# An MLP in rounds of 1024 inner channels, its up steps placed among another round's down steps

## The chip, the cores and the metric

The kernel runs on one core of a Trainium2 chip. The metric is the device time of one execution in microseconds; a run's time is the median over repeated executions on the same chip.

## The reference, cut to what matters

One layer on 256 tokens of width 2048, all in float32: a chunked gated linear attention mixer, then a squared-ReLU MLP with 8192 inner channels, then a last RMS norm.

```python
h = h + _gla_mixer(_rmsnorm(h, gla_norm[0]), ...)
a = jax.nn.relu(_rmsnorm(h, mlp_norm[0]) @ w_up)     # 256 x 8192
h = h + (a * a) @ w_down                             # 256 x 2048
return _rmsnorm(h, final_norm)
```

## The kernel before, in words

Every product is made from float32 split in two parts of the type float32r, a high part (ScalarE casts) and a low part (VectorE subtracts the cast from the value). A product is the sum of three matmuls: high by high, high by low, low by high. Nearly all matmuls are 128 x 128 by 128 x 256. Weights come from memory as raw tiles through SP's queue, 512 KB to a load; `parts` (or `weights`) splits a raw tile into a slot `hi` and a slot `lo`, of which there are five each. The raw tiles were held in three pairs.

The order of the instructions on each engine is fixed when the program is built, by a scheduler that follows the program's text and its own estimate of when things are ready; each engine then works its list in order and waits on semaphores. The list `side` holds small jobs that `pump` puts between the steps of the main loops.

The mixer takes about the first 375 us. Then the MLP follows in four rounds of 2048 inner channels (`ROUNDS = HID // D`):

- `up(r, q, act)`, four blocks of 512 channels. `turned` runs 8 steps (kp) for each block; a step loads 256 x 512 of `w_up` and makes 24 matmuls, with the weights as the stationary operand and the transposed hidden state (`hth`, `htl`) as the moving one. Then ReLU and square, and for each bank of 256 channels the eight forms of the activation that the down steps use: the four quarters A11, A12, A21, A22 (two token halves by two channel tiles) and the four combinations S1 to S4, split into high and low parts.
- `down(r, half, act)`, two half passes over 1024 of the 2048 output columns, each 8 steps (kp) over 256 channels. The left 512 columns go by sums: seven products of 256 columns in place of eight (Winograd's form of Strassen's scheme), for which VectorE forms four sums of the weights (`u`, three additions) that are split as well. The right 512 columns are plain, in 24 matmuls. `blocks` are the plain products, `product` the others. At the end of a half pass the banks are added into `h` (`take`) and into `sums`.

In the last round the second half pass is replaced by a plain loop over 16 channel tiles at the end, whose last six weights are held so that the output columns can be finished one after the other.

"Even" steps: TensorE's operands lie so that stationary tiles start at 192 bytes past a multiple of 256 (`OFF = 48`), moving ones at a multiple. In a step with `gap` set the second half of the weights is moved by 64 bytes:

```python
between = SLOT - OFF - 2 * GT if gap else 0
to = [a[:, OFF - between : OFF + 2 * GT + between].rearrange("p (i c) -> p i c", i=2)[:, :, between:] for a in to]
```

Of the kernel before, what the change touches and what calls it, by code (L numbers as in the profile page):

```python
# [27 lines left out]
F32 = mybir.dt.float32  # L28
# [33 lines left out]
ROUNDS = HID // D  # L62
# [5 lines left out]
def tile_gla_mlp(ctx, tc, x, xt, cols, w_vg, w_in, w_gate, w_out, w_up, w_down, final_norm, out):  # L68
# [7 lines left out]
    st = ctx.enter_context(tc.tile_pool(name="st", bufs=4))  # L76
# [37 lines left out]
    raw_half = []  # L114
# [5 lines left out]
    def weights(src, n, pieces=None, room=None, skip=0, raw=None, gap=None):  # L120
# [3 lines left out]
        if raw is None:  # L124
            if not raw_half:
                raw_half.extend(raw_pair())
            raw = raw_half.pop(0)
        loads, pieces = pieces or ([(0, n)], [(skip, n)])
# [43 lines left out]
    def turned(row, w, c0, even=(0,), acc=None):  # L172

        acc = acc or acc_banks(GT // P // 2)
        for kp in range(KT // 2):
            wh, wl = weights(w[2 * kp * P : 2 * (kp + 1) * P, c0 : c0 + GT].rearrange("(i p) c -> p i c", p=P), 2 * GT, gap=kp in even)
            for i in range(2):
                kt = 2 * kp + i
                ah, al = row(kt)
                for j in range(GT // P):  # L180
                    s = slice(j * P, (j + 1) * P)
                    o = acc[j // 2][:, j % 2 * T : (j % 2 + 1) * T]
# [6 lines left out]
                if kt < KT - 1:  # L189
                    pump()  # L190
        return acc
# [25 lines left out]
    mhalf = const.tile([P, 1], F32, name="mhalf")  # L217
# [18 lines left out]
    xe = mid.tile([P, 2, 2, P], F32R, tag="xe", name="xe")  # L236
# [98 lines left out]
    gn = const.tile([P, NT, GR], F32, name="gn")  # L335
# [19 lines left out]
    gt = mid.tile([GR, T], F32R, tag="gt", name="gt")  # L355
# [248 lines left out]
    sums = [big.tile([P, 4, T], F32, tag="E" + i, name="sums", bufs=1) for i in "hl"]  # L604
    turned_h = lambda kt: [a[:, kt, :].rearrange("p (t s) -> p t s", t=NT) for a in (hth, htl)]
# [30 lines left out]
    A11, A12, A21, A22, S3, S1, S2, S4 = range(8)  # L636
    KP = KT // 2
# [4 lines left out]
    def up(r, q, act):  # L642
        acc = turned(lambda kt: (hth[:, kt], htl[:, kt]), w_up, r * D + q * GT, even=() if q > 1 or r > 0 and q else (6,) if r == q == 0 else (0,))
        flush()
        f = work[:, 2].rearrange("p (f s) -> p f s", f=8)
        for b in range(2):
            s = tmp.tile([P, 2, T], F32, tag="t512", name="su", bufs=3)
            nc.vector.scalar_tensor_tensor(
                s, acc[b].rearrange("p (i t) -> p i t", i=2), 0.0, r2row.unsqueeze(1).to_broadcast([P, 2, T]),
                op0=ALU.max, op1=ALU.mult,  # L650
            )
            nc.scalar.activation(
                f[:, :4].rearrange("p (t i) s -> p i t s", t=2), s.rearrange("p i (t s) -> p i t s", t=2), AF.Square
            )
            sub = lambda o, x, y: nc.vector.tensor_tensor(o, x, y, op=ALU.subtract)
            sub(f[:, S3 : S1 + 1], f[:, A21 : A21 + 1].to_broadcast([P, 2, P]), f[:, A11 : A22 + 1 : 3])
            sub(f[:, S2], f[:, A11], f[:, S1])
            sub(f[:, S4], f[:, A12], f[:, S2])
            oh, ol = (act[q][:, b, i].rearrange("p f s -> p (f s)") for i in range(2))
            nc.scalar.copy(oh, work[:, 2])  # L660
            nc.vector.tensor_tensor(ol, work[:, 2], oh.bitcast(F32), op=ALU.subtract)

    def stationary(act, kp, f):
        return [act[kp // 2][:, kp % 2, i, f] for i in range(2)]
# [4 lines left out]
    def down(r, half, act):  # L669

        c0 = half * G
        plain = [aux_bank(), aux_bank()] if half == 0 else acc_banks(2)
        b32, b74 = acc_banks(2) if half == 0 else [aux_bank(), aux_bank()]
# [176 lines left out]
```

## Time and profile before

| | us |
|---|---|
| median of three runs | 1070.55 (1070.04 to 1071.04) |
| the profiled execution | 1070.33 |
| its span, first to last instruction | 1068.2 |
| TensorE busy in it | 1059.3 |
| VectorE busy | 780.7 |
| ScalarE busy | 579.9 |

The profile is of one execution. PE is TensorE, DVE VectorE, ACT ScalarE, POOL GpSimd, SP the engine that issues most loads. A row of the groups has the line, engine and operation, what is written and read, the count, then busy time and the mean duration of one in ns, then the idle time in front of them and what ended it. A row of the windows has a stretch of the span, its length, and for each engine its busy time and the number of instructions in it, then TensorE's granted clock, the DMA share and GB/s. A row of the timeline has start, duration, engine, line and operation. Matmuls overlap, so their own durations (0.28 us) say less than the distance of their starts.

### The profile page before, as it was taken

The page shows a single profiled execution, that of the slowest core. Times are in us where ns is not written, and L with a number is a line of the kernel's source. Part 1 is how long each engine was busy: PE and PEld are TensorE (multiplying, and loading weights), DVE is VectorE, ACT ScalarE, POOL GpSimd, SP SyncE. Part 2 cuts the span into 40 slices and gives each one's busy share as a digit, 9 for nine tenths or more (in the row PEclk, how much of TensorE's full clock was granted, in tenths as well). Part 3 has the DMA queues.
Part 4 walks back from the last instruction along what each step waited for, and adds up shares of the span by engine and source line. Part 5 has one row for each costly group of instructions (what it writes and reads, how often), then busy time and mean ns, then how long its engine had stood idle before and what let it go on. Part 6 is the DMA issues. An engine that isn't in the chain of part 4 may idle for free.

```text
span 1068.2 us, 21835 instructions
## 1 busy us (share of the span) xinstructions
PE 1059.3 (99%) x9262; PEld 1058.8 (99%) x9262; DVE 780.7 (73%) x1041; ACT 579.9 (54%) x701; POOL 12.8 (1%) x39
## 2 busy tenths in 40 slices
PE   9999999999999999999999999999999999999997
PEld 9999999999999999999999999999999999999996
DVE  5777645656555566789976689986779997778984
ACT  6775444546445455556654456554556554555652
POOL 0000000000000000000000000000000000000000
PEclk9999999999999999999999999999999999999999
DMA  9857665555555555556575655566655666665662
GB/s 340 301 165 233 195 191 155 161 150 178 198 179 179 196 172 186 195 167 228 198 236 183 198 174 200 198 223 211 198 197 165 196 233 217 193 192 177 219 227 79
DMA packets 79425, 210.43 MB, mean 197 GB/s; under 512 B 6704, under 2 KB 7600, under 8 KB 79200
## 3 DMA queue, kind: packets, MB, share of 16 engines
q1 hardware_dynamic: 78368, 206.99, 59.3%
q10 hardware_dynamic: 960, 2.05, 0.5%
q8 instruction: 72, 1.18, 0.4%
q14 instruction: 25, 0.20, 0.1%
HBM read 206.92 MB, written 2.10 MB: 196 GB/s over the span
## 4 chain that ended last, share of the span: by engine, by line
PE 98%; issue 1%; DVE 0%; ACT 0%; POOLq 0%; POOL 0%; DVEq 0%; ACTq 0%
PE acc L148 44%; PE acc L185 39%; PE aux L148 12%; PE aux L185 2%; PE aux L546 1%; PE aux L474 1%; PE aux L211 0%; PE acc L375 0%; DVE hf L809 0%; ACT sqf L762 0%; DVE h L667 0%; POOLq L846 0%; POOL rf L309 0%; PE aux L628 0%; DVEq L846 0%
## 5 line engine op out<-in xcount | busy, mean ns | idle before, releaser
L111 DVE TENSOR_TENSOR lo<-raw,hi 128x768 fp32r<-128x768 f32 (+3 forms) x226 | 257.0, 1138 | 120.2 <-ACT hi L110 118.1
L110 ACT CAST hi<-raw 128x768 fp32r<-128x768 f32 (+3 forms) x226 | 222.1, 984 | 214.0 <-PE acc L148 130.7
L185 PE MATMUL acc<-hh,hi 128*128 128x256 f32 x1024 | 283.2, 277 | 0.0
L185 PE MATMUL acc<-hl,hi 128*128 128x256 f32 x1024 | 283.2, 277 | 0.0
L185 PE MATMUL acc<-hh,lo 128*128 128x256 f32 x1024 | 283.1, 276 | 0.0
L137 DVE TENSOR_TENSOR lo<-raw,hi 128x1024 fp32r<-128x1024 f32 x160 | 195.3, 1223 | 110.1 <-ACT hi L136 109.0
L136 ACT CAST hi<-raw 128x1024 fp32r<-128x1024 f32 x160 | 167.9, 1051 | 181.1 <-PE acc L185 141.6
L148 PE MATMUL acc<-hi,act 128*128 128x256 f32 x1200 | 218.1, 276 | 0.0
L185 PEld LDWEIGHTS acc<-hh,hi 128*128 128x128 f32 x1024 | 192.3, 188 | 0.0
L185 PEld LDWEIGHTS acc<-hl,hi 128*128 128x128 f32 x1024 | 192.3, 188 | 0.0
L185 PEld LDWEIGHTS acc<-hh,lo 128*128 128x128 f32 x1024 | 192.3, 188 | 0.0
L148 PEld LDWEIGHTS acc<-hi,act 128*128 128x128 f32 x1200 | 180.9, 188 | 0.0
L148 PE MATMUL acc<-lo,act 128*128 128x256 f32 x600 | 143.3, 276 | 0.0
L148 PE MATMUL aux<-hi,act 128*128 128x256 f32 x704 | 133.8, 276 | 0.0
L148 PEld LDWEIGHTS aux<-hi,act 128*128 128x128 f32 x704 | 106.5, 188 | 0.0
L148 PE MATMUL acc<-hi,xA 128*128 128x256 f32 (+1 forms) x736 | 105.0, 280 | 0.0
L148 PEld LDWEIGHTS acc<-lo,act 128*128 128x128 f32 x600 | 102.5, 188 | 0.0
L148 PEld LDWEIGHTS acc<-hi,xA 128*128 128x128 f32 x736 | 94.0, 189 | 0.2 <-ACT hi L110 0.2
L110 ACT CAST hi<-work 128x1024 fp32r<-128x1024 f32 x56 | 59.1, 1056 | 38.3 <-PE aux L148 14.2
L148 PE MATMUL aux<-lo,act 128*128 128x256 f32 x352 | 76.4, 276 | 0.0
L111 DVE TENSOR_TENSOR lo<-work,hi 128x1024 fp32r<-128x1024 f32 x56 | 68.3, 1219 | 9.7 <-ACT hi L110 7.7
L148 PE MATMUL acc<-lo,xA 128*128 128x256 f32 (+1 forms) x368 | 58.6, 278 | 0.0
(162 smaller groups left out, 1271.8 us busy)
## 6 DMA issues: line engine op xcount, KB each, us to landing
raw<-in_w_up SPq DMA_DIRECT2D x128, 512.0 KB, 4.3
raw<-in_w_down SPq DMA_DIRECT2D x128, 512.0 KB, 4.4
raw<-in_w_in SPq DMA_DIRECT2D x80, 512.0 KB, 4.8
raw<-in_w_out SPq DMA_DIRECT2D x32, 512.0 KB, 4.1
raw<-in_w_vg SPq DMA_DIRECT2D x14, 520.0 KB, 8.8
h<-in_x SPq DMA_DIRECT2D x4, 512.0 KB, 7.6
zz<-in_xt SPq DMA_DIRECT2D x3, 384.0 KB, 8.5
fb<-in_final_norm ACTq DMA_DIRECT2D x1, 1024.0 KB, 6.8
```

What stands on the lines that cost most here:

```text
L110: last_hi[0] = nc.scalar.copy(hi[:, s], raw[:, s])
L111: last_lo[0] = nc.vector.tensor_tensor(lo[:, s], raw[:, s], hi[:, s].bitcast(F32), op=ALU.subtract)
L136: last_hi[0] = nc.scalar.copy(to[0], dst)
L137: last_lo[0] = nc.vector.tensor_tensor(to[1], dst, to[0].bitcast(F32), op=ALU.subtract)
L148: nc.tensor.matmul(o[:, m], x, w[:, m], start=first and c == 0, stop=last, skip_group_check=True)
L185: nc.tensor.matmul(o, u[:, i, s], m, start=kt == 0 and n == 0 and j % 2 == 0, stop=kt == KT - 1 and n == 2, skip_group_check=True,)
L474: nc.tensor.matmul(o, kab[:, k[0], c0 + c, k[1] : k[1] + P], q(qt[:, c0 + c]), start=c == 0, stop=c == 1)
L546: nc.tensor.transpose(b[:, o + t * P : o + (t + 1) * P], src[:, t, kt * P : (kt + 1) * P], ident)
```

## The change

The MLP goes in eight rounds of 1024 inner channels. `up` and `down` have become generators: 18 up steps run first (the first round's 16 and two more), and from then on each down step is followed by one up step of the next round, until the up steps are used up.

A down pass is now over one group of 512 output columns and one round (4 steps of 256 channels). A step is either plain (24 matmuls) or by sums (21) for all of its 512 columns; `by_sums` says which: three of four steps, two of four for group 1 and in the round before the last, and two steps in all in the last round. The groups are taken in one order and in the reverse in turn, so that the last group of one round is the first of the next and its four banks stay open. `sums` has four tiles instead of two; the small additions that end a group (`combine`) go to `side`. The first up block uses two of the six `acc` banks, the others the two `aux` banks.

There are six raw tiles of one step each instead of three pairs. The activation's forms are kept in another order, and those that no step uses are not made. Some small tiles are moved or padded in SBUF (`mhalf`, `gn`, `xe` and `gt` in one tile), which leaves the starts of TensorE's operands at the same offsets within 512 bytes. The plain loop at the end is over 8 channel tiles instead of 16. The even steps of the MLP are kp 6 and kp 0 of the first round's two blocks and kp 3 of each later round's first block.

```diff
-ROUNDS = HID // D
+MR = 2 * GT
+ROUNDS = HID // MR
...
-    st = ctx.enter_context(tc.tile_pool(name="st", bufs=4))
+    st = ctx.enter_context(tc.tile_pool(name="st", bufs=3))
...
-    def raw_pair():
-        a = wpool.tile([P, 2 * WMAX], F32, tag="raw", name="raw", bufs=3)
-        return a[:, :WMAX], a[:, WMAX:]
+    def raw_tile():
+        return wpool.tile([P, WMAX], F32, tag="raw", name="raw", bufs=6)
...
-    def turned(row, w, c0, even=(0,), acc=None):
-        acc = acc or acc_banks(GT // P // 2)
+    def turned_steps(row, w, c0, even, acc, flip=0):
         for kp in range(KT // 2):
...
+            yield
...
+    def by_sums(m, g, kp):
+        if m == ROUNDS - 1:
+            return (g, kp) in ((1, 0), (1, 2))
+        return kp < (2 if g == 1 or m == ROUNDS - 2 else 3)
+
+    def up():
+        for m in range(ROUNDS):
+            for q in range(MR // GT):
+                first = m == q == 0
+                acc = acc_banks(2) if first else [aux_bank(), aux_bank()]
+                even = (6,) if first else (0,) if m == 0 else (3,) if q == 0 else ()
+                yield from turned_steps(lambda kt: (hth[:, kt], htl[:, kt]), w_up, m * MR + q * GT, even, acc, 1)
...
+    def down(passes):
+        for n, (m, g) in enumerate(passes):
+            if not n or passes[n - 1][1] != g:
+                b32, bx4, b16, b57 = acc_banks(4)
+            ends = n + 1 == len(passes) or passes[n + 1][1] != g
+            for kp in range(KP):
...
+                raw = raw_tile()[:, : 2 * GT]
+                src = w_down[c0 : c0 + 2 * P, g * GT : (g + 1) * GT].rearrange("(i p) c -> p i c", p=P)
+                last_load[0] = nc.sync.dma_start(out=raw.rearrange("p (i c) -> p i c", i=2), in_=src)
+                if not by_sums(m, g, kp):
+                    w = parts(raw, 2 * GT, slots())
+                    for i in range(2):
+                        for bank, f in ((b32, (A11, A12)), (bx4, (A21, A22))):
+                            product(bank, slice(0, GT), at(f[i]), w, slice(i * GT, (i + 1) * GT))
+                    yield
+                    continue
+                w = parts(raw, 2 * GT, slots(), [(T, 2 * GT)])
...
+                add(u[:, :2], raw[:, :1].to_broadcast([P, 2, T]), raw[:, 1:3])
+                add(u[:, 2], u[:, 0], raw[:, 2])
+                add(u[:, 3], u[:, 2], raw[:, 3])
+                wu = parts(wk, G, slots())
+                product(b16, left, at(A11), w, block(1))
+                product(b32, right, at(A12), w, block(3))
+                product(b32, left, at(S4), w, block(2))
+                product(b57, left, at(S1), wu, block(0))
+                product(b57, right, at(S3), wu, block(1))
+                product(b16, right, at(S2), wu, block(2))
+                product(bx4, right, at(A22), wu, block(3))
+                yield
+            if ends:
+                take(b32, 0, g * GT, GT)
+                take(bx4, 1, g * GT, GT)
...
+    passes = [(m, g) for m in range(ROUNDS) for g in order_of(m) if m < ROUNDS - 1 or g < 2]
+    steps = up()
+    for _ in range(KT + 2):
+        next(steps)
+    for _ in down(passes):
+        next(steps, None)
...
-    acc = [acc_banks(len(cuts[t])) for t in range(NT)]
+    acc = [[aux_bank(), aux_bank()], acc_banks(3)]
+    KL = MR // P
...
-    for kt in range(KT):
+    for kt in range(KL):
```

More of the change, by code (lines that the diff above doesn't have):

```diff
@@ L640, in tile_gla_mlp @@
     work = work[:, : 3 * G].rearrange("p (b c) -> p b c", b=3)
[L642 to L654 removed]
+    acts = [[None] * (KP // 2) for _ in range(ROUNDS)]
```

189 lines of the change are left out of this document (87 added, 102 removed).

## The prediction

> **What bounds the kernel now.** I read the page from the top, then the chain that ended last, then windows over the MLP, then single rows of TensorE and of VectorE.
>
> ```profile
> span 1068.2 us, 21835 instructions
> PE 1059.3 (99%) x9262; PEld 1058.8 (99%) x9262; DVE 780.7 (73%) x1041; ACT 579.9 (54%) x701; POOL 12.8 (1%) x39
> ...
> 551.46 87.12 PE acc L185 x768
> ...
> 552.89:721.61 168.72, 168.72 (x1490) 168.72 (x1489) 138.20 (x182) 92.82 (x97) 0.00 (x0) 1.00 0.61 200
> 640.00:700.00 60.00, 60.00 (x532) 60.00 (x531) 59.00 (x84) 36.83 (x40) 0.00 (x0) 1.00 0.59 200
> ```
>
> TensorE is busy for 99% of the span. The chain shows 768 up-projection matmuls in 87.12 us without a wait, so one matmul costs 113.4 ns here. The first window is one whole round of before: 168.72 us hold the 1488 matmuls of 2048 channels (113.4 ns each), VectorE is busy for 138.2 us (82%). The second window lies in its down steps: VectorE 59.0 of 60, and TensorE still lost nothing. So time follows the number of matmuls, with VectorE close behind it.
>
> A second thing belongs to the bound: the pitch of the matmuls has two values.
>
> ```profile
> 383.85 1.03 PE L546 MATMUL aux<-ident,h 128*128 128x128 f32 x8
> ...
> 384.84 0.28 PE L185 MATMUL acc<-hl,hi 128*128 128x256 f32 x1
> ...
> 391.32 0.28 PE L185 MATMUL acc<-hh,lo 128*128 128x256 f32 x1
> ...
> 405.81 0.28 PE L185 MATMUL acc<-hl,hi 128*128 128x256 f32 x1
> ...
> 407.25 0.28 PE L185 MATMUL acc<-hl,hi 128*128 128x256 f32 x1
> ```
>
> After the eight short transposes at 383.85 the next 55 matmuls take 6.48 us, 117.8 ns each instead of 113.4, and stay so until an "even" step, whose shifted half runs 12 matmuls in 1.44 us (120 ns, the last two rows); behind it the pitch is 113.4 again. So an interruption of TensorE costs its own length and then 4.4 ns on every matmul up to the next even step. The MLP of before has no such interruption after its first up block.
>
> **The change, part by part.**
>
> *Matmuls.* A plain step over 256 channels and 512 columns has 4 x 2 x 3 = 24 matmuls, one by sums 21. Before, 7 half passes of 8 steps are by sums: 56. After, rounds 0 to 5 have 3+2+3+3 = 11 steps by sums of 16, round 6 has 8, round 7 has 2: 76. Twenty more steps save 3 matmuls each: 60, and the order of the built programs agrees (9228 to 9168). 60 x 113.4 ns = **-6.80 us**. All of them lie on the path, since TensorE is it.
>
> *Even steps.* Five in the MLP before (one of kp 6, one of the first round's second block, one in each of three rounds), nine after. Each costs 12 x (120 - 113.4) = 0.08 us: **+0.32 us**.
>
> *VectorE.* It gets the work that TensorE loses, so I count a round of 1024 channels of after.
>
> ```profile
> L137 DVE TENSOR_TENSOR lo<-raw,hi 128x1024 fp32r<-128x1024 f32 x160 | 195.3, 1223 | 110.1 <-ACT hi L136 109.0 <-PE aux L546 0.6
> L111 DVE TENSOR_TENSOR lo<-work,hi 128x1024 fp32r<-128x1024 f32 x56 | 68.3, 1219 | 9.7 <-ACT hi L110 7.7
> L111 DVE TENSOR_TENSOR lo<-raw,hi 128x768 fp32r<-128x768 f32 x56 | 53.4, 953 | 4.6 <-ACT hi L110 3.4
> L700 DVE TENSOR_TENSOR work<-work,raw 128x256 f32<-128x256 f32 x112 | 46.7, 417 | 0.2
> L700 DVE TENSOR_TENSOR work<-raw 128x512 f32<-128x512 f32 x56 | 38.3, 684 | 1.5 <-DMA raw<-in_w_down 1.3
> L648 DVE SCALAR_TENSOR_TENSOR su<-acc,work 128x512 f32<-128x512 f32 x32 | 21.1, 688 | 0.0
> L655 DVE TENSOR_TENSOR work<-work 128x128 f32<-128x128 f32 x64 | 18.6, 290 | 1.6
> L655 DVE TENSOR_TENSOR work<-work 128x256 f32<-128x256 f32 x32 | 13.4, 418 | 0.0
> L667 DVE TENSOR_TENSOR h<-acc,h 128x512 f32<-128x512 f32 x13 | 8.7, 684 | 7.2 <-PE acc L148 7.2
> L136 ACT CAST hi<-raw 128x1024 fp32r<-128x1024 f32 x160 | 167.9, 1051 | 181.1 <-PE acc L185 141.6 <-issue 17.5 <-PE acc L148 17.1
> L110 ACT CAST hi<-raw 128x768 fp32r<-128x768 f32 x56 | 47.0, 839 | 56.4 <-PE aux L148 27.9 <-PE acc L148 15.2 <-PE acc L185 13.3
> ...
> 993.52 1.22 DVE L111 TENSOR_TENSOR lo<-raw,hi 128x1024 fp32r<-128x1024 f32 x1
> 994.66 0.42 DVE L700 TENSOR_TENSOR work<-work,raw 128x256 f32<-128x256 f32 x1
> 994.99 1.22 DVE L111 TENSOR_TENSOR lo<-work,hi 128x1024 fp32r<-128x1024 f32 x1
> ```
>
> A step by sums costs 953 + 684 + 2 x 417 + 1219 = 3.69 us of vector instructions, a plain or an up step 1.22. Sixteen up steps 19.6, eleven by sums 40.6, five plain 6.1; the four activation banks 9.8 (four times 688, three times 418 + 2 x 290, and low parts of 896, 896, 1024 and 512 columns, the first two put at 1.09 us, halfway between the 768 and 1024 rows); three group ends of four 512-column additions, 8.2. Sum 84.3 us in 105 instructions. TensorE has 384 + 231 + 120 = 735 matmuls = 83.3 us. But queued vector instructions start before the one in front has ended: the last three rows start 1.14 and 0.33 us apart where they last 1.22 and 0.42, so each gives 0.08 us back. 84.3 - 105 x 0.082 = **75.7 us of 83.3**. Between the two ways of counting, the round of before (148.8 us by durations, 133.9 by starts) showed 138.2. I take the starts, as the lower bound of what VectorE needs when it is pressed: it is not the bound by itself, with 7.6 us to spare per round.
>
> The Trainium skill ("VectorE: DVE Perf Modes", section "The DRAIN you can't avoid") says the next operation does not start until the pipe has emptied; by that the need would be the full 84.3. The same page (section "Two Vector instructions with no wait between them") says that one that is not held starts earlier, and the rows above agree with that.
>
> *The raw tiles: what eats the spare 7.6 us.* The adds of a step by sums read the raw tile itself, and the order of the built program puts the first of them three to four steps ahead. That tile's buffer was freed only shortly before, by the low split of the load six tiles back, and the load that fills it waits in SP's queue for that split. I summed the vector work between the two, in starts: before, at least 4.2 us in all 56 cases, and VectorE waited 1.3 us for DMA in all (row L700 above). After: under 2 us in 3 of 76 cases, 2 to 3 in 27 (two splits of 1.14, for instance), 3 to 4 in 20, more in 26. Against this stands the landing time of a load.
>
> ```profile
> L133 SPq DMA_DIRECT2D raw<-in_w_up x1: 368/368/368, 567.4 to 567.4; - x1
> ...
> DMA to landing us min/median/max: 3.7/3.7/3.7
> ...
> DMA to landing us min/median/max: 3.7/4.2/4.6
> ...
> DMA to landing us min/median/max: 3.5/4.2/6.0
> ```
>
> The first two are one load of the pair issued at 567.4, the third both loads of that pair, the fourth all loads between 552.89 and 721.61. Before frees two raw tiles at once and issues in pairs, and the second of a pair lands last (4.6). After frees them singly, so I take the first's 3.7 us (its rows are of 2 KB, as those of w_down become), and 0.1 us for issue and wake-up. Adding up max(0, 3.8 - work) over the eleven adds of a round gives 4.9 to 6.8 us of waiting by round: 75.7 + 6.8 = 82.5 at most, still under 83.3, with under 1 us to spare. At a landing of 3.9 it is even; at the median 4.2 (4.3 with wake-up) the waits are 8.4 to 11.2 us and the round 84.1 to 86.9, over TensorE's 83.3. While VectorE waits at an add, the splits behind it wait too, and TensorE lives on the five weight slots.
>
> The Trainium skill ("DMA: Bandwidth & Descriptors", section "Anatomy of one DMA — SWDGE (gpsimd) path") gives 2.0 us and the bytes at 436 GB/s, 3.2 us for such a load as an estimate; here 3.5 is the shortest, and by 3.2 the waits would be no danger. Its "Rules for kernel authors" speak against the change: issue early, wait late. Here the wait moves closer to the issue, and the result hangs on it.
>
> Some loads land late (6.0 in the last row). I allow one that reaches TensorE: about 0.5 us, and half a round at the slow pitch, 367 x 4.4 ns = 1.6 us. Zero to **+2.1 us**; I take half, 1.05.
>
> *Hand-offs.* Up blocks now share two aux banks: the next block's first matmul waits for the two ReLU instructions (2 x 0.61 us in starts), with a down step of at least 21 x 113.4 ns = 2.4 us between. A new column group writes its b16 into the bank of the last b32, which one addition (0.60) must have emptied, with an up step (2.7 us) between. Both are covered while VectorE keeps pace; without that cover each of some 38 places costs up to 1.2 us.
>
> *At nothing.* ScalarE: 16 + 5 casts of 1051 ns, eleven pairs of 839 and 1051, and some 6 us for the activations make 49 us of a round's 83.3. Loads and bytes stay as many. The steps ahead of the MLP keep their order but for one raw load moved ahead of an input load; TensorE idles 8.9 us in the whole span (1068.2 - 1059.3), most of it at both ends, so I put the bounds at -0.5 and +0.5 us. The end keeps its last six held weights and the chain behind the last matmul, but only two steps instead of ten stand ahead of them: from the last group's start TensorE takes 90 + 48 + 30 matmuls, 19.1 us, until it wants the last split; VectorE has two steps by sums, two plain ones, eight splits and four additions there, 2 x 3.28 + 10 x 1.14 + 4 x 0.60 = 20.4 us in starts, and comes with a lead of up to five slots (five splits, 5.7 us). Covered; 1.3 us if the lead is gone.
>
> Sum: -6.80 + 0.32 + 1.05 = -5.43 us. The profiled execution took 1070.33 us (2.1 outside its span), so 1064.9 by its own time; the median of the runs is 1070.55, 0.2 above: 1070.55 - 5.43 = **1065.1 us**.
>
> **The rivals.** *The loads decide, in most rounds.* If a single load takes 4.2 us as the median does, VectorE falls behind, TensorE pauses at the group starts, and each pause drops the pitch until the round's one even step; then a round takes up to 735 x 117.8 ns = 86.6 us instead of 83.3. Over seven rounds at half to full effect +11.5 to +23 us, less 6.5: 1075.5 to 1087. It decides from a landing of about 4.0 us. For it: the median 4.2. Against: the first of a pair, 3.7. *The same in two to four rounds only:* +4 to +9 less 6.5, 1068 to 1073. *The pipe empties after each vector instruction:* 84.3 + 4.9 to 6.8 of waits is 89 to 91 us a round against 83.3, +6 to +8 in each of seven, 1105 to 1119. The start times speak against it. (It is the rule of the Trainium skill's "VectorE: DVE Perf Modes" weighed above.) *The change doesn't do what it says:* each of the 23 group ends pauses 0.3 us and returns the 6.8, 1070; no such wait showed at before's seven half passes.
>
> **How the numbers follow.** Forecast 0.60; loads in most rounds 0.20; in some 0.15; the last two 0.05 together. This kernel's measurement tells 0.2% (2.1 us) from no change. Faster by more means under 1068.4: the forecast and half of the third, 0.67. Within: the rest of the third and the 1070 case, 0.11. Slower 0.22. The range runs from 1063.3 (no late load, the early part 0.5 better) to 1075, the lower end of the loads' case, and leaves out about 2 in 10.
>
> **What would show it.** 9202 matmul records; a whole round of 83 to 84 us; VectorE at 94% or more there; waits of the adds for DMA of about 5 us a round where before had 1.3 in all. Wrong, if the chain shows TensorE waiting on VectorE in the MLP, if 60 us there hold about 512 matmuls (117.8 ns) where the second window above has 532, or if the landing of w_down loads has a median over 4.0 us.

## The result, and the profile after

The changed kernel takes 1079.49 us (median; 1077.17 to 1084.84), the kernel before 1070.32 in the same runs: ratio 1.0091, 95% interval 1.0069 to 1.0114. It is slower by 9.2 us where 5.4 us less were forecast. The profiled execution is the slowest of the six, 1084.84 us, 14.5 above the one of before; what follows from its trace is about that execution, and the median's 9.2 us were not traced.

The page of the changed kernel: span, busy times, the chain by engine and line, the groups of TensorE's up and down matmuls and of the adds, and the loads with their median time to landing.

```profile
span 1082.5 us, 22093 instructions
PE 1068.2 (99%) x9202; PEld 1066.8 (99%) x9202; DVE 831.1 (77%) x1144; ACT 587.9 (54%) x723; POOL 12.8 (1%) x39
PE 83%; DMA 7%; DVE 7%; issue 2%; ACT 0%; SPq 0%; DVEq 0%; POOLq 0%; POOL 0%; ACTq 0%
...
L180 PE MATMUL aux<-hh,hi 128*128 128x256 f32 x960 | 266.5, 278 | 2.8 <-DVE su L676 2.8
...
L143 PE MATMUL acc<-lo,act 128*128 128x256 f32 x908 | 223.0, 278 | 2.2 <-DVE lo L112 2.2
...
L736 DVE TENSOR_TENSOR work<-raw 128x512 f32<-128x512 f32 x76 | 52.5, 690 | 48.0 <-DMA raw<-in_w_down 47.7
...
raw<-in_w_up SPq DMA_DIRECT2D x128, 512.0 KB, 3.8
raw<-in_w_down SPq DMA_DIRECT2D x128, 512.0 KB, 4.3
```

The 60 matmuls are gone (9262 to 9202). The busy share still says 99%, and it hides the loss: a matmul at the slower pitch counts as busy. What is new is DMA and VectorE in the chain, 48 us of waiting at the first add of the steps by sums (1.5 us before), and TensorE waiting for `su` (the ReLU that empties an aux bank) and for low parts, 5 us in all.

Windows of 60 us over the changed kernel's MLP, TensorE first with its matmuls:

```profile
460.00:520.00 60.00, 59.30 (x505) 59.10 (x504) 53.38 (x74) 35.02 (x42) 0.00 (x0) 1.00 0.62 194
520.00:580.00 60.00, 60.00 (x529) 60.00 (x528) 52.95 (x72) 33.83 (x38) 0.00 (x0) 1.00 0.63 197
...
640.00:700.00 60.00, 60.00 (x512) 60.00 (x511) 53.91 (x75) 33.31 (x37) 0.00 (x0) 1.00 0.66 197
...
880.00:940.00 60.00, 57.82 (x492) 57.42 (x491) 53.15 (x76) 32.02 (x35) 0.00 (x0) 1.00 0.62 191
940.00:1000.00 60.00, 60.00 (x512) 60.00 (x511) 50.33 (x68) 31.49 (x35) 0.00 (x0) 1.00 0.63 192
```

Two windows here are full and still hold only 512 matmuls, whose starts are 117.8 ns apart, with the granted clock at 1.00 (two or three of the 512 lie partly outside). Two have real pauses. How two of them come about, in VectorE's timeline of the changed kernel and in TensorE's rows behind the pauses:

```profile
886.58 0.69 DVE L736 TENSOR_TENSOR work<-raw 128x512 f32<-128x512 f32 x1 [3.27 <-DMA raw<-in_w_down]
887.19 1.22 DVE L132 TENSOR_TENSOR lo<-raw,hi 128x1024 fp32r<-128x1024 f32 x1
...
891.27 1.28 DVE L760 TENSOR_TENSOR sums<-acc,sums 128x512 f32<-128x512 f32 x2
892.47 1.22 DVE L112 TENSOR_TENSOR lo<-raw,hi 128x1024 fp32r<-128x1024 f32 x1
895.45 0.69 DVE L736 TENSOR_TENSOR work<-raw 128x512 f32<-128x512 f32 x1 [1.76 <-DMA raw<-in_w_down]
896.06 1.22 DVE L132 TENSOR_TENSOR lo<-raw,hi 128x1024 fp32r<-128x1024 f32 x1
897.19 1.28 DVE L676 SCALAR_TENSOR_TENSOR su<-aux,work 128x512 f32<-128x512 f32 x2
```

```profile
888.46 0.38 PE L180 MATMUL aux<-hh,lo 128*128 128x256 f32 x1 [0.16 <-DVE lo L132]
...
897.93 0.38 PE L180 MATMUL aux<-hh,hi 128*128 128x256 f32 x1 [2.02 <-DVE su L676]
```

The first add stands 3.27 us for its load, the split behind it is late, and TensorE pauses 0.3 us at 888.1; from there on its matmuls come at the slower pitch. The second add stands 1.76 us. Behind it are a split and the two ReLU instructions without which TensorE may not write the aux banks again: TensorE pauses 2.2 us at 895.7, and the pitch stays slow. All five pauses of over 0.3 us in this trace are like that: TensorE is let go by a split or by `su`, and 1.9 to 2.5 us earlier VectorE began an add that had waited 0.8 to 3.3 us for a load of `w_down`.

Nearly the whole loss of the profiled execution lies in the MLP and can be added up from the starts of its matmuls. "MLP" is from its first up matmul to the end of the last matmul: 680.57 us before, 694.31 after, +13.74. The matmuls and even steps give -6.80 + 0.32. Five pauses (two starts over 0.3 us apart; the pause is what goes beyond one pitch) make 6.0, smaller ones 0.6, and 3232 matmuls at the slower pitch where before had 137 make 3095 x 4.45 ns = 13.8: sum 13.9. Another 0.5 us is lost ahead of the MLP.

### The profile page after: what moved, and what is told of

Read it like the earlier page. It is cut to its first block, busy times and chain, and to the rows that moved or that the text cites. A ratio compares the mean times of both kernels' runs of the same rounds, so it can differ in the third digit from the quotient of the medians.

```text
span 1082.5 us, 22093 instructions
## 1 busy us (share of the span) xinstructions
PE 1068.2 (99%) x9202; PEld 1066.8 (99%) x9202; DVE 831.1 (77%) x1144; ACT 587.9 (54%) x723; POOL 12.8 (1%) x39
## 4 chain that ended last, share of the span: by engine, by line
PE 83%; DMA 7%; DVE 7%; issue 2%; ACT 0%; SPq 0%; DVEq 0%; POOLq 0%; POOL 0%; ACTq 0%
PE acc L143 45%; PE aux L180 26%; PE acc L180 8%; DMA raw<-in_w_down 5%; DVE lo L112 3%; PE aux L143 2%; DVE lo L132 1%; DVE work L736 1%; DMA raw<-in_w_vg 1%; PE aux L549 1%; DMA zz<-in_xt 1%; DVE h L698 1%; PE aux L477 1%; DVE sums L760 0%; DVE su L676 0%
## 5 line engine op out<-in xcount | busy, mean ns | idle before, releaser
L143 PE MATMUL acc<-hi,act 128*128 128x256 f32 x1816 | 319.4, 278 | 0.0
L143 PEld LDWEIGHTS acc<-hi,act 128*128 128x128 f32 x1816 | 269.9, 188 | 0.0
L180 PE MATMUL aux<-hh,hi 128*128 128x256 f32 x960 | 266.5, 278 | 2.8 <-DVE su L676 2.8
L180 PE MATMUL aux<-hh,lo 128*128 128x256 f32 x960 | 266.7, 278 | 0.2 <-DVE lo L132 0.2
L180 PE MATMUL aux<-hl,hi 128*128 128x256 f32 x960 | 266.5, 278 | 0.0
L143 PE MATMUL acc<-lo,act 128*128 128x256 f32 x908 | 223.0, 278 | 2.2 <-DVE lo L112 2.2
L180 PEld LDWEIGHTS aux<-hh,hi 128*128 128x128 f32 x960 | 180.1, 188 | 3.2 <-DVE su L676 3.2
L180 PEld LDWEIGHTS aux<-hh,lo 128*128 128x128 f32 x960 | 180.3, 188 | 0.4 <-DVE lo L132 0.4
L180 PEld LDWEIGHTS aux<-hl,hi 128*128 128x128 f32 x960 | 180.2, 188 | 0.0
L736 DVE TENSOR_TENSOR work<-raw 128x512 f32<-128x512 f32 x76 | 52.5, 690 | 48.0 <-DMA raw<-in_w_down 47.7
L736 DVE TENSOR_TENSOR work<-work,raw 128x256 f32<-128x256 f32 x152 | 63.9, 420 | 1.0
L143 PEld LDWEIGHTS acc<-lo,xA 128*128 128x128 f32 x368 | 49.8, 188 | 0.3 <-DVE lo L112 0.3
```

The costliest lines, as they stand in the source:

```text
L143: nc.tensor.matmul(o[:, m], x, w[:, m], start=first and c == 0, stop=last, skip_group_check=True)
L180: nc.tensor.matmul(o, u[:, i, s], m, start=kt == 0 and n == 0 and j % 2 == 0, stop=kt == KT - 1 and n == 2, skip_group_check=True,)
L736: add = lambda o, x, y: nc.vector.tensor_tensor(o, x, y, op=ALU.add)
```

## The experiments

The theories named in the expectations: A, the loads of `w_down` land later than the adds want them; VectorE waits with what is queued behind, TensorE pauses and goes on at the slower pitch. B, VectorE has too much work, whatever it waits for. C, the slower pitch comes from the interleaving. D, the six single tiles are the cause. E, a late load stops TensorE whatever VectorE's spare time. In the table the median is of all runs and the rest is from that kernel's profiled execution, which lies up to 5.4 us from its median: the adds' wait for DMA in the whole kernel, the pauses of TensorE over 0.3 us and the matmuls at the slower pitch, both in the MLP, and its length. "Raw 4 + 2" means four raw tiles for `w_down` and two for `w_up`. The freeing split of a load is VectorE's last reading of the raw tile that the load will overwrite.

| kernel | median, us | adds' wait | pauses, us | slow matmuls | MLP, us |
|---|---|---|---|---|---|
| before | 1070.3 | 1.3 | 0 | 137 | 680.6 |
| changed | 1079.5 | 47.7 | 5, 6.0 | 3232 | 694.3 |
| adds later | 1091.9 | 0 | 13, 6.0 | 3686 | 698.1 |
| more even steps | 1077.9 | 49.8 | 6, 8.2 | 921 | 688.5 |
| no even steps | 1085.9 | 40.9 | 2, 1.0 | 4566 | 694.6 |
| raw pairs | 1073.7 | 44.4 | 1, 0.8 | 1841 | 683.0 |
| raw 4 + 2 | 1069.7 | 20.1 | 2, 0.7 | 1416 | 680.6 |
| raw 4 + 2, more even | 1068.4 | 21.9 | 1, 1.4 | 291 | 676.8 |
| sums not added | 1086.4 | 49.4 | 4, 5.2 | 2921 | 692.0 |
| 58 steps by sums | 1096.9 | 66.8 | 10, 7.2 | 3882 | 705.2 |
| raw 3 + 2 | 1082.3 | 44.9 | 4, 5.1 | 2984 | 694.0 |
| four slots, raw 5 + 3 | 1073.7 | 1.6 | 0 | 501 | 675.9 |
| five then four slots, raw 5 + 3 | 1072.1 | 2.1 | 0 | 192 | 674.4 |
| five then four slots, raw 3 + 3 | 1094.9 | 60.6 | 6, 3.2 | 4977 | 700.3 |
| the last but one, fifth slot aligned | 1065.9 | 1.8 | 0 | 135 | 674.1 |

**The adds later.**

```diff
+                before = last_lo[0]
                 w = parts(raw, 2 * GT, slots(), [(T, 2 * GT)])
 ...
+                with tc.issue_after(before.ins):
                     add(u[:, :2], raw[:, :1].to_broadcast([P, 2, T]), raw[:, 1:3])
                     add(u[:, 2], u[:, 0], raw[:, 2])
                     add(u[:, 3], u[:, 2], raw[:, 3])
```

> The three adds of a by-sums step are put behind the split that VectorE did just before this step's own; at least 8.0 us of vector work (by the durations of the trace) then lies between the split that frees a raw tile and the first add on its new content, where it was 1.1 to 7.2 us. Work and sums are the same. Theory A (the loads land later than the early adds want them, VectorE waits with its splits queued behind, TensorE pauses and falls to the slower pitch): the adds' waits for w_down fall from 47.7 us to under 3, no pause of TensorE over 0.3 us is left in the MLP, the pitch stays at 113.4 ns, and the time is the prediction's sum, 1064 to 1066 us. Theory B (VectorE has too much work with 20 more steps by sums, whatever it waits for): 1077 to 1080 us, unchanged. Theory C (the slower pitch comes from the interleaving of up and down steps itself): pauses go, the 117.8 ns stretches stay, about 1073 us.

Measured 1091.9 us (1.0188, 1.0167 to 1.0210): none of the three. The waits for DMA are gone as built, and others are in their place. VectorE's two longest waits between 440 and 960 us in the changed kernel (us, times, longest), the longest in this one, and a piece of this one's timeline:

```profile
DVE work L736 <- DMA raw<-in_w_down: 44.8, 41, 3.3
DVE lo L112 <- ACT hi L111: 13.1, 15, 2.0
```

```profile
DVE lo L112 <- ACT hi L111: 46.7, 53, 1.2
```

```profile
590.16 0.88 DVE L737 TENSOR_TENSOR work<-work,raw 128x256 f32<-128x256 f32 x2
591.56 1.40 DVE L676 SCALAR_TENSOR_TENSOR su<-aux,work 128x512 f32<-128x512 f32 x2 [0.53 <-PE aux L180]
592.88 1.22 DVE L112 TENSOR_TENSOR lo<-work,hi 128x1024 fp32r<-128x1024 f32 x1
```

The split of the sums now stands right behind the adds that make them (68 of 76 with under 1.2 us of vector work between, 39 in the changed kernel), so VectorE waits for ScalarE's cast, 46.7 us where it was 13.1, and TensorE's pauses end with ScalarE's casts (8) or with splits (5). The early place of the adds had a use; taking a wait away by moving its instruction only moved it. This run does not decide between A and B, and A's own figure missed as well.

**More even steps, and none.**

```diff
-                even = (6,) if first else (0,) if m == 0 else (3,) if q == 0 else ()
+                even = (6,) if first else (0,) if m == 0 else (3,)
```

> One more even step in each round from the second on, in the second half of the up steps (seven in all, 12 matmuls at 120 ns each, 0.08 us a step); order and sums unchanged. Theory A: the adds' waits (about 48 us) and the pauses (five, about 6.5 us in all) stay, but a slow stretch ends about 42 us earlier; of the 3084 slow matmuls of the profiled run some 750 to 1300 are left, that is 8 to 10 us less than in that run and, since it was the slowest of six, 5 to 9 us less than the median: 1071 to 1075 us. Theory B: the time stays at 1077 to 1080 us, whatever the pitch, since TensorE would only wait longer for VectorE.

and with `()` in place of `(3,) if q == 0 else ()`:

> The even steps of the rounds from the second on are taken out (seven); order and sums unchanged. Theory A: after the first pause, near 465 us, TensorE stays at 117.8 ns to the end: some 5000 slow matmuls instead of 3084 in the profiled run, 8 to 10 us more than that run, less 0.56 us for the even steps: 1086 to 1093 us. Theory B: 1077 to 1080 us, unchanged.

Measured 1077.94 us (1.0075, 1.0062 to 1.0087) and 1085.86 (1.0149, 1.0134 to 1.0165). With more even steps the slow matmuls fall to 921 as expected, but the median falls by 1.6 us and not by 5 to 9, and the two intervals overlap. In the two traces, both of executions above their medians, the MLP is 5.8 us shorter: the pitch gives back 2311 x 4.45 = 10.3 us, the added even steps cost 0.6, the pauses grow from 6.0 to 8.2 us, and behind the longest of them the granted clock is at 0.50 for 3.4 us, about 1.5 us more. That TensorE waits longer because it wants its weights sooner at the faster pitch is likely, not shown.

Without even steps the pitch falls at 551.9 us and never comes back; TensorE's rows there, and two windows:

```profile
551.50 0.28 PE L143 MATMUL acc<-lo,act 128*128 128x256 f32 x1
551.65 0.39 PE L180 MATMUL aux<-hh,hi 128*128 128x256 f32 x1
551.88 0.28 PE L180 MATMUL aux<-hl,hi 128*128 128x256 f32 x1
```

```profile
460.00:520.00 60.00, 60.00 (x532) 60.00 (x532) 54.59 (x76) 37.49 (x43) 0.00 (x0) 1.00 0.63 200
760.00:820.00 60.00, 60.00 (x512) 60.00 (x512) 53.30 (x74) 34.03 (x38) 0.00 (x0) 1.00 0.64 193
```

The two starts at 551.65 and 551.88 are late by 0.16 us together. That is no pause by the table's limit, and it was enough; the two pauses of the table, 1.0 us together, come later, when the pitch is already slow. The median lies just under the 1086 to 1093 expected. So the price of the pitch is real (4566 slow matmuls, 20 us), and it follows pauses, very short ones too, and not the interleaving: up to 551 us up and down steps alternate here at 113.4 ns (against C).

**Raw tiles in pairs again.**

```diff
-        return wpool.tile([P, WMAX], F32, tag="raw", name="raw", bufs=6)
+        if not raw_half:
+            a = wpool.tile([P, 2 * WMAX], F32, tag="raw", name="raw", bufs=3)
+            raw_half.extend((a[:, :WMAX], a[:, WMAX:]))
+        return raw_half.pop(0)
```

> One part of the change undone: the raw weight tiles are three pairs again and not six single tiles, so loads are issued two at a time, once both tiles are free; sums and rounds as in the changed kernel. In the built order 40 of the 76 by-sums steps have under 4 us of vector work between the freeing split and the first add (2.0 to 7.3 us in all). Theory A: the adds still wait, 40 to 60 us in all, and the time stays within 1074 to 1082 us. Rival D (the six single tiles are what made the loads late): the waits are near 2 us, as in the kernel before, and the time is 1064 to 1067 us.

Measured 1073.72 us (1.0033, 1.0021 to 1.0046). That is 0.3 us under A's range. The adds still wait 44 us, so D falls; but there is one pause over 0.3 us instead of five, and three of 0.1 to 0.3 us at which the pitch fell. How much is waited doesn't tell where it is waited.

**Four raw tiles for `w_down`, two for `w_up`.**

```diff
-        return wpool.tile([P, WMAX], F32, tag="raw", name="raw", bufs=6)
+        n_raw[0] += 1
+        down = kind == "down" if kind else n_raw[0] % 6 < 4
+        return wpool.tile([P, WMAX], F32, tag="raw" + "ud"[down], name="raw", bufs=4 if down else 2)
```

(`kind` is "down" or "up" in the MLP and none ahead of it, where the six take turns.)

> The six raw tiles are shared out by kind in the MLP: four for w_down and two for w_up (in the changed kernel the two kinds take turns, three each). Work, sums, even steps and bytes are the same. In the built order 15 of the 76 by-sums steps have under 4.0 us of vector work between the freeing split and the first add (50 in the changed kernel), and 61 have over 4. Theory A (a round on VectorE is its work, some 76.5 us, and its waits for loads, 8.2 us: 85 us against TensorE's 83.3, so TensorE is made to pause): the adds' waits fall from 47.7 to 15 to 25 us, a round of VectorE to under 81 us, the pauses go, and the time is 1064 to 1067 us. Theory B (VectorE's work alone is too much, and waits only take the place of other idling, as with the late adds): the waits turn up elsewhere on VectorE and the time stays over 1073 us.

> The last kernel with one more even step in each round from the second on (0.08 us each, 0.56 us in all). Theory A: without pauses there is nothing to repair, so 0.3 to 0.6 us more than the kernel with four and two; if one or two pauses are left, up to 3 us less. Theory B: as the kernel with four and two, over 1073 us.

Measured 1069.73 us (1.0004, 0.9989 to 1.0018) and 1068.37 (0.9986, 0.9975 to 0.9996). Same memory, work and bytes as the changed kernel, and 9.8 us less: fewer late loads, fewer pauses. It misses 1064 to 1067 by what two pauses of 0.7 us together leave behind, 1279 slow matmuls more than before had, 5.7 us; with the added even steps 291 are left, and one pause of 1.4 us at 967.

**VectorE relieved, loads left late; and fewer steps by sums.**

```diff
-                    if g not in begun:
-                        nc.scalar.copy(dst, b)
-                    else:
-                        nc.vector.tensor_tensor(dst, b, dst, op=ALU.add)
+                    nc.scalar.copy(dst, b)
```

> VectorE is relieved and the loads are left as they are: the sums' banks are copied by ScalarE in every round and not added by VectorE in rounds after the first, so this kernel leaves out the accumulation of the sums over the rounds (its output is not the reference's; TensorE's work is unchanged). VectorE loses two adds of 128x512 a group, some 5 us a round. In the built order the adds stand as close behind their loads as in the changed kernel or closer (56 of 76 with under 4.0 us of vector work). Theory A: the adds' waits stay at 45 to 65 us, but a round of VectorE is 80 to 82 us and TensorE does not pause for it: 1064 to 1068 us. Rival E (one late load stops TensorE directly, whatever VectorE's spare): pauses stay and the time is 1074 us or more.

```diff
-        return kp < (2 if g == 1 or m == ROUNDS - 2 else 3)
+        return kp < 2
```

> The number of by-sums steps is taken back nearly to what it was, in every group two of four: 58 steps instead of 76, so 54 matmuls more, 6.1 us, and some 2.5 us of vector work less for each step not taken, 6 to 7 us a round. The adds stand closer behind their loads than in the changed kernel (44 of 58 with under 4.0 us of vector work). Theory A: the waits stay near 8 to 12 us a round, but VectorE has 70 us of work, so a round is 80 to 82 us of TensorE's 84.2: few pauses and 1069 to 1072 us. Rival E: pauses as before, 1080 us or more.

Measured 1086.44 us (1.0144, 1.0127 to 1.0160) and 1096.92 (1.0256, 1.0234 to 1.0279). Both are far over A's figures, and on E's side; the first of them leaves out the adding of the sums over the rounds. The busy times of the kernel that doesn't add the sums, a piece of VectorE's timeline in it, and the page of the kernel with 58 steps by sums:

```profile
PE 1066.0 (99%) x9202; PEld 1064.6 (99%) x9202; DVE 812.4 (75%) x1106; ACT 607.0 (56%) x761; POOL 12.8 (1%) x39
```

```profile
722.76 0.69 DVE L736 TENSOR_TENSOR work<-raw 128x512 f32<-128x512 f32 x1 [3.31 <-DMA raw<-in_w_down]
723.37 1.22 DVE L132 TENSOR_TENSOR lo<-raw,hi 128x1024 fp32r<-128x1024 f32 x1
724.51 0.42 DVE L736 TENSOR_TENSOR work<-work,raw 128x256 f32<-128x256 f32 x1
724.84 1.28 DVE L676 SCALAR_TENSOR_TENSOR su<-aux,work 128x512 f32<-128x512 f32 x2
```

```profile
PE 1078.9 (99%) x9256; PEld 1076.2 (98%) x9256; DVE 787.5 (72%) x1054; ACT 573.0 (52%) x705; POOL 12.8 (1%) x39
...
L736 DVE TENSOR_TENSOR work<-raw 128x512 f32<-128x512 f32 x58 | 40.1, 691 | 66.9 <-DMA raw<-in_w_down 66.8
```

VectorE has 19 and 44 us less to do than in the changed kernel (831.1), and TensorE still pauses 5.2 and 7.2 us, where it was 6.0. In the first kernel the relief was smaller than the 5 us a round that I had put down (38 additions less, 19 us in all). But B falls: the kernel with the least vector work is the slowest, and the last kernel below has 836.5 us of it and no pause. In the rows at 722 the add waits 3.31 us, since the split in front of it is the one that freed its tile; two instructions on stands `su`, and TensorE pauses 2.7 us there. What VectorE has to spare over a round does not help at that place: `su` can't be done ahead, because its bank is full only when TensorE has ended the up block, one down step before TensorE wants the bank again.

**Five raw tiles, three and two.**

```diff
-        return wpool.tile([P, WMAX], F32, tag="raw", name="raw", bufs=6)
+        n_raw[0] += 1
+        down = kind == "down" if kind else n_raw[0] % 5 < 3
+        return wpool.tile([P, WMAX], F32, tag="raw" + "ud"[down], name="raw", bufs=3 if down else 2)
```

> Five raw tiles instead of six: three for w_down, as many as in the changed kernel, and two for w_up. In the built order the distances of the adds are those of the changed kernel to within a tile or two (49 of 76 with under 4.0 us of vector work, 50 there). If the adds' loads decide and w_up's third tile buys nothing: waits of the adds 42 to 52 us, four to six pauses, 1077 to 1083 us. If the number of raw tiles as such decides: clearly slower than the changed kernel, 1085 us or more.

Measured 1082.26 us (1.0113, 1.0099 to 1.0126), within what was expected if the loads of `w_down` decide. Against these five tiles, a fourth for `w_down` is worth 12.5 us (1069.7). A third for `w_up`, the changed kernel, shows no clear gain: its runs of 1077.2 to 1084.8 us and these of 1080.7 to 1084.4 overlap, and the two MLPs take 694.3 and 694.0 us.

**Four slots, and eight raw tiles.**

```diff
-    wpool = ctx.enter_context(tc.tile_pool(name="wpool", bufs=5))
+    wpool = ctx.enter_context(tc.tile_pool(name="wpool", bufs=4))
 ...
+        return wpool.tile([P, WMAX], F32, tag="raw" + "ud"[down], name="raw", bufs=5 if down else 3)
```

> Late loads are taken away by another way: four slots for split weights instead of five, and with the memory two raw tiles more, five for w_down and three for w_up. In the built order 5 of the 76 by-sums steps have under 4.0 us of vector work between the freeing split and the first add. Work and sums are the same, and VectorE's spare time in a round is larger by the waits, but its lead over TensorE is a slot shorter (a step by sums fills two slots). If the lead decides what a delay costs (a wait of 2 to 3 us, or VectorE's own bunches of work at a group's end, against a lead of a few us): pauses come back though the adds' waits are under 8 us, and the time is 1075 us or more. If late loads alone decide: no pauses over 0.3 us and 1064 to 1067 us.

Measured 1073.67 us (1.0032, 1.0020 to 1.0043): neither figure, since both looked at the MLP alone. In the MLP there is no pause over 0.3 us, 675.9 us against 694.3. But TensorE arrives there 7.2 us later (387.4 instead of 380.2): at 22 us of the span it waits 5.7 us for ScalarE's cast, ScalarE having stood 10.3 us for a load (4.4 in the changed kernel), and the granted clock is at 0.50 for 6.8 us from 24.8 on. That it is the missing fifth slot which delays that load is likely, not shown. The shorter lead costs no pause in the MLP.

**Five slots ahead of the MLP, then four.** The memory of the fifth pair of slots becomes two raw tiles for `w_down` from the second round of up steps on; the second kernel leaves it unused.

```diff
+        n_slots[0] += 1
+        fifth = not rounds[0] and n_slots[0] % 5 == 0
+        return [wpool.tile([P, SLOT], F32R, tag=i + "5" * fifth, name=i, bufs=1 if fifth else 4) for i in ("hi", "lo")]
 ...
+        if kind == "down":
+            n_down[0] += 1
+            if n_down[0] % 5 > 2:
+                return wpool.tile([P, SLOT], F32, tag=("hi5", "lo5")[n_down[0] % 5 - 3], name="raw", bufs=1)[:, :WMAX]
+        return wpool.tile([P, WMAX], F32, tag="raw" + "ud"[down], name="raw", bufs=3)
```

> Before the MLP five slots and six raw tiles, as in the changed kernel; from the second round of up steps on four slots, and the memory of the fifth is two more raw tiles: five for w_down, three for w_up. In the built order 6 of 76 by-sums steps have under 4.0 us of vector work between the freeing split and the first add. Work, sums and even steps are those of the changed kernel. If late loads were the whole loss: waits of the adds under 5 us, no pause over 0.3 us, the pitch at 113.3 to 113.4 ns all through the MLP, which starts at 385 us and not at 392 us as in the kernel with four slots throughout; by the sum of the prediction, 1063.5 to 1066 us. If the changed form has another cost yet: over 1068 us.

> As the last kernel, but the two raw tiles in the memory of the fifth slot are left unused: three raw tiles for w_down, three for w_up, four slots in the MLP. 48 of 76 by-sums steps have under 4.0 us of vector work between the freeing split and the first add. If the loads of w_down decide: the adds wait 45 to 60 us in all, pauses and slow stretches are back, 1076 to 1086 us, some 12 to 20 us above the last kernel by nothing but two raw tiles. If the four slots are what made the kernel with four slots throughout free of pauses: as the last kernel.

Measured 1072.12 us (1.0016, 1.0007 to 1.0025) and 1094.93 (1.0230, 1.0216 to 1.0244). The first lies over the 1063.5 to 1066 expected, the second 9 us over its range of 1076 to 1086. This pair is the clearest of the study: two raw tiles apart, 22.8 us. It is not apart in the tiles alone, for with other tiles the scheduler also orders 139 of VectorE's 1144 instructions otherwise, and some of TensorE's steps; what that does by itself is not known. But in the slower one too, each of the six pauses stands 1.3 to 5.4 us behind an add that had waited 0.9 to 3.3 us for its load. VectorE's waits between 440 and 960 us, first with five tiles for `w_down`, then with three:

```profile
DVE lo L116 <- ACT hi L115: 34.1, 56, 1.9
...
DVE lo L116 <- DMA raw<-in_w_down: 0.3, 2, 0.2
```

```profile
DVE work L745 <- DMA raw<-in_w_down: 56.5, 40, 3.3
DVE lo L116 <- ACT hi L115: 3.5, 6, 1.1
```

With three, VectorE waits for loads; with five, for ScalarE's casts, and these in turn for slots that TensorE has still to free: VectorE is ahead. With three the MLP takes 700.3 us, 25.9 more than with five, and 4785 more slow matmuls are 21.3 of that. With five it takes 674.36 us, without a pause. That the whole was 1072.1 and not 1063.5 to 1066 is the other cost that the expectation allowed for, and it lies ahead of the MLP, which starts at 386.5 us instead of 380.2 (the expectations count the start 5.4 us later, behind the eight short transposes).

**The fifth slot aligned.** Its pair began 128 bytes past a multiple of 256 where the other four begin at a multiple; 32 unused elements move it.

```diff
+        pad = {i: 32 if fifth and i == "hi" else 0 for i in ("hi", "lo")}
+        return [wpool.tile([P, pad[i] + SLOT], F32R, tag=i + "5" * fifth, name=i, bufs=1 if fifth else 4)[:, pad[i] :] for i in pad]
```

> The kernel with five slots before the MLP and five raw tiles for w_down in it, with one difference: the fifth slot of the high parts begins 128 bytes further on, so that the first bytes of all ten slots have the same remainder by 256 as in the changed kernel (in the kernel before this one the fifth pair stood 128 bytes off). Order, sums, waits and sizes are the same. If the slower pitch before the MLP comes from that offset: the slow stretches of 12 matmuls before the MLP fall from 196 to about 86 as in the changed kernel, the MLP starts at 385 us and not 391.5 us, and the time is 1064.5 to 1066.5 us. If it comes from something else in the sharing of the memory: 1071 to 1073 us as before.

Measured 1065.85 us (1065.51 to 1066.53), ratio 0.9959 (0.9946 to 0.9973): faster than both kernels, as expected. A window ahead of the MLP, first unaligned, then aligned, and one row of the aligned kernel's MLP:

```profile
180.00:240.00 60.00, 60.00 (x515) 60.00 (x514) 33.45 (x46) 29.15 (x46) 4.40 (x8) 1.00 0.52 153
```

```profile
180.00:240.00 60.00, 60.00 (x526) 60.00 (x525) 33.33 (x47) 29.11 (x44) 4.39 (x8) 1.00 0.53 153
...
760.00:820.00 60.00, 60.00 (x531) 60.00 (x530) 57.00 (x80) 35.78 (x38) 0.00 (x0) 1.00 0.68 204
```

Eleven matmuls more in the same 60 us, by 128 bytes; the instructions and their order are the same in both. And in the MLP 531 in 60 us with VectorE at 57.0 of 60: the full pace that the prediction had counted on.

## Why the prediction was wrong, step by step

**Matmuls and even steps: right, to the hundredth.** The last kernel has the changed kernel's matmuls, sums and even steps. Its MLP takes 674.09 us against 680.57 before: -6.48, which is -6.80 + 0.32. The sum is confirmed; that two single executions agree with it to the hundredth is luck.

**VectorE's need: right.** In the last kernel it is busy 93% of the time between 580 and 880 us (279.5 of 300) and TensorE is not held: 77.6 us of a round of 83.3, near the 75.7 taken and well under the 84.3 by durations. The rival by which the pipe empties after each instruction is ruled out: by it the instructions alone would take 84.3 us of each round of 83.3. So the rule of the Trainium skill's "VectorE: DVE Perf Modes" (section "The DRAIN you can't avoid"), taken without its own note that an instruction which is not held starts earlier, does not hold here.

**The raw tiles: the step that failed, in its size and in its reasoning.** The size: a single load was put at 3.7 us because the first of a pair took that. In the changed kernel the loads of `w_down` land after 4.3 us in the median. The first of a pair had nothing issued shortly before it; in the changed kernel 102 of the 128 loads of `w_down` are issued less than 3 us behind another (numbers below). None of the MLP's loads there landed within the 3.2 us at which the prediction saw no danger; the shortest took 3.5. So 44.8 us were waited at the adds between 440 and 960 us, 7.5 us in 87, where 4.9 to 6.8 a round were forecast. The reasoning: those waits were summed over a round and held against the round's spare 7.6 us. By that measure even 7.5 us would just have been hidden. But at `su`, and where VectorE had no lead, a wait of 1.8 to 3.3 us went straight to TensorE, in the changed kernel and in one with less vector work. Slack at another time is no cover. What counted was the distance between the freeing split and the add at the few places where TensorE is next in line. That the landing time alone does not decide is shown by the pages of before, of the changed kernel and of the last one:

```profile
raw<-in_w_down SPq DMA_DIRECT2D x128, 512.0 KB, 4.4
...
raw<-in_w_down SPq DMA_DIRECT2D x128, 512.0 KB, 4.3
...
raw<-in_w_down SPq DMA_DIRECT2D x128, 512.0 KB, 4.6
```

The loads land latest in the kernel whose adds wait 1.8 us in all: there 6 of the 76 adds stand under 4.0 us of vector work behind the freeing split, in the changed kernel 50.

**The late load that was allowed: right in kind, wrong in number.** One pause, then the slower pitch until the round's even step, 1.05 us. There were five pauses, and the pitch cost twice as much as they did (13.8 against 6.0 us), behind 957 us because the even step did not bring the pitch back.

**Hand-offs:** "covered while VectorE keeps pace" was the right condition. It didn't keep pace, and the aux banks are where two of the five pauses, the two with 2.8 us of idle time between them, were taken.

**At nothing:** ahead of the MLP 0.5 us was lost, the bound that was given; the end is the same to 0.1 us.

**The rivals.** "The loads decide, in most rounds" (1075.5 to 1087, from a landing of about 4.0 us) is what happened in time, at 0.20; the pitch was slow in part of five of the seven rounds, so it stands between this rival and the one of two to four rounds. All three signs of being wrong that the prediction named came: TensorE waiting on VectorE, 512 matmuls in 60 us, and a median landing over 4.0 us, though the last does not tell the kernels apart. The later landing was already in a row that the prediction shows, the median of 4.2, and the forecast set it aside for the 3.7 of a position in the queue that the change abolishes. The rule of the Trainium skill's "DMA: Bandwidth & Descriptors" (section "Rules for kernel authors") that was set against the change, to issue early and wait late, is borne out by the pair with five and three tiles, 1072.1 against 1094.9 us.

What is not settled: how much of each difference is due to the order that the scheduler builds for other buffers; why the pauses fell from five to one with pairs, at nearly the same waits, was not taken apart, and the 1.2 us that the last kernel loses ahead of the MLP and 1.1 us behind it were not looked into.

## What to carry to other kernels

When a change lets an engine work closer behind its loads, list for each load the instruction that frees its buffer and the first that reads it, and hold the work between the two against the landing time that such a load has in the new rhythm of issues (4.3 to 4.6 us in the median here, not the 3.7 of the quickest position); a sum over a round against the round's slack hides the few places that cost. Buffers are worth most where that distance is shortest: the same six tiles shared four to two, not three to three, gave back 9.8 us, and eight, with the fifth slot aligned, gave all. And on TensorE look at the matmuls in a window, not at the busy share, which said 98 or 99% in all fifteen kernels. Where late loads decide, one trace is one draw: the runs of the three changed kernels without a pause over 0.3 us lie within 1.8 us of one another, those of the kernels with pauses up to 8.5 us apart.

## What the runs showed of the hardware that was not expected

- A 512 KB load's landing goes with how long before it another was issued on the queue. From the issue records of the changed kernel between 440 and 960 us, medians: 4.5 us at 0.6 to 1.2 us behind another, 5.1 at 1.2 to 1.8, 4.3 at 1.8 to 2.2, 4.0 at 2.2 to 2.6, 3.8 at 3.0 to 3.6, 3.7 beyond. In the kernel with four and two tiles and more even steps, the last of four loads issued within 4.4 us took 6.2 us, and VectorE waited 4.55 us for it.
- A pause too short for the table lowers the pitch, and not every pause does. Behind 410 us of the fourteen traces after the change, 42 times a distance of over 150 ns between two starts met TensorE at 113.4 ns, with 0.08 to 2.8 us lost; 40 times it went on at 117.8. A pause of 2.0 us at 722.9 in the kernel with more even steps left the pitch alone.
- An even step does not always bring the faster pitch back. In the changed kernel's last round the 12 shifted matmuls at 957.0 us came with distances of 117, 118 and 125 ns among the 120, and the pitch stayed at 117.8 to the end; at 528, 699 and 786 us it came back.
- A long pause can lower the granted clock. In the kernel with more even steps it was at 0.50 for 3.4 us behind the pause of 2.6 us at 894.2, with matmuls 213 ns apart; pauses of 2.2 us in the changed kernel and 2.7 us in the one that doesn't add the sums left it at 1.00.

```profile
898.40:901.60 3.20, 3.20 (x17) 3.20 (x16) 3.20 (x8) 0.12 (x1) 0.00 (x0) 0.50 0.72 244
```

- The start of one slot of five, 128 bytes off, was enough to lower the pitch ahead of the MLP: some 110 groups of twelve matmuls more than in the changed kernel took over 115 ns each, and the MLP started 6.2 us later.
